# A pool of six buffers for the gates, split off from the common pool

## The chip, the cores and the metric

The kernel runs on one core of one Trainium2 chip. The metric is the time of one execution on the device, in microseconds (us). The kernel is one decoder block over 512 positions, in float32 accuracy.

## What is computed

The reference, cut to what matters here (`D_MODEL` = 1024, `D_CONV` = 1024, `D_RNN` = 1280, `D_FF` = 2816):

```python
z = rmsnorm(x, norm1_g) @ w_in + b_in
z_glu, z_rx, z_rg, z_ga, z_gb = split(z)
u = causal_conv31(glu(z_glu)); y_a = silu(layernorm(u)) @ conv_w_out + conv_b_out
xb = causal_conv4(z_rx)
r, i = sigmoid(xb @ wa + ba), sigmoid(xb @ wx + bx)      # 16 blocks of 80 x 80
log_a = -8 * r * softplus(-lam); a = exp(log_a)
h[t] = a[t] * h[t-1] + sqrt(-expm1(2 * log_a))[t] * (i * xb)[t]
y_b = (h * gelu(z_rg)) @ lru_w_out
x = x + (sigmoid(z_ga) * y_a + sigmoid(z_gb) * y_b) @ w_mix_out
h2 = rmsnorm(x, norm2_g)
x = x + (silu(h2 @ w1) * (h2 @ w3)) @ w2                 # SwiGLU
out = rmsnorm(x, norm_f_g)
```

## The kernel before, in words

**Tiles and buffers.** Activations lie channel by position, in tiles of 128 x 512 float32. Each such tile takes a buffer of the pool "long" (65 buffers, `SLOTS`) or, if it lives briefly, of "short" (5). A buffer is taken at the first write of a tile and is free again after the last read. A float32 product is made of three matmuls of rounded parts (`mm3`, line 428): every operand is split into a high part, cast on ACT (line 117), and a low part, the difference, on DVE or POOL (line 113). A split thus takes two "long" buffers (`pairt`, line 97) for one tile.

**Weights** come in chunks: a load into one of 4 raw buffers, a cast on ACT, a subtraction on POOL (for `w_in` and the gates' weights) or on DVE (for all later ones), into one of 5 buffers "hl". `weights` (line 161) emits them 4 chunks ahead of the product that uses them.

**Order.** The program states what is computed from what; a planner in the framework fixes, when the program is built, the order of the instructions on each engine, which buffer each tile takes, and the waits. It goes through the program with estimates of its own for the durations, prefers what stands earlier in the program, and lets an instruction that needs a buffer wait until one is free. On the chip each engine goes through its own list in that order.

**Stages.** (1) `norm1` and the transposes to `h1` (8 pairs of tiles, 16 buffers). (2) A list `ORDER` (line 201) mixes the input products (`z`, line 437), the gates `g0` to `g9` (`gates`, line 702), the recurrences `r0` to `r9` (`recur`, line 736) and, in steps between them, the 31 taps of the long convolution on DVE (line 596). In the list each `r` follows its `g` so that at most three gates are open: g0, g1, g2, then r0 and r1, and so on. (3) `yb`, 8 products over the 10 pairs `y`; beside them the layer norm of the convolution, and sums of weight blocks for the mixing product (`make_sums`, line 276) whose splits `mxt1k`, `mxt4k` stay in "long". (4) `ya`, and the mixing product `mx` with seven block products instead of eight (`Sevenfold`, line 806). (5) `norm2` to `h2`, then the two SwiGLU products, `f` and, for four of eleven pairs, `fr`. (6) The last product `or` (Sevenfold again, named "o", line 842), and the final norm.

**The gates.** `gates(j)` makes two products into PSUM banks `r_` and `i_`, and from them, with ACT and DVE, two tiles that outlive it, `th{j}` (line 721) and `ea{j}` (line 725). `recur(j)` reads `th{j}` in a square root on ACT (line 739) and `ea{j}` in the scan on DVE (line 741). These are "the gates' two lasting results".

**Sevenfold pairs.** For each of the 11 pairs of column blocks of the SwiGLU result, `pair(k, ua, va)` (line 821) leaves five "long" tiles: the split of `u` (`ous{k}`, two buffers), the split sum `os1p{k}`, the differences `oe{k}` (line 829) and `ov{k}`. `run` (line 842) then goes over the pairs a first time: product `k` reads `ous{k}` and `os1p{k}` (line 840), which frees three buffers, and the pair's later operands are split off, `oe{k}` to `oeb{k}` and `ov{k}` to `ovb{k}` (line 863), which takes four and frees two. These `oeb` and `ovb` are needed only in the second pass over the pairs. After pair 0 `run` also starts the loads of the residual `x2b` (8 buffers) and of the last norm's weights `gf` (2 buffers).

Of the kernel before, what the change touches and what calls it, by code (L numbers as in the profile page):

```python
# [28 lines left out]
NF = DF // P  # L29


SLOTS, SHORT = 65, 5
RAW = 4
HL = 5
AHEAD = 4
# [45 lines left out]
def tile_block(ctx, tc, a, out):  # L81
# [9 lines left out]
    def tiles(tag, bufs):  # L91
        p_ = pool(tag, bufs)
        return lambda name, dtype=F32: p_.tile([P, T], dtype, tag=tag, name=name)

    longt, shortt = tiles("long", SLOTS), tiles("short", SHORT)

    def pairt(name, dtype=F32R):

# [2 lines left out]
    def bank(name):  # L101
        return psum.tile([P, T], F32, tag="mm", name=name)
# [9 lines left out]
    def sub(eng, o, x, y):  # L112
        return eng.tensor_tensor(out=o, in0=x, in1=y, op=ALU.subtract)  # L113

    def split_to(h, l, full, eng, copy=act.copy):

        copy(h, full)  # L117
        last = sub(eng, l, full, h.bitcast(F32))
        if eng is pool_e:
            newest["sub"] = last.ins  # L120
        return h, l

    def split(name, full, eng, p_=None, copy=act.copy):
        p_ = p_ or pairt(name)
        return split_to(*p_, full, eng, copy)
# [35 lines left out]
    def weights(key, ahead=AHEAD):  # L161
        i = next(i for i, c in enumerate(chunks) if c[0] == key)
        emit_to(i + 1 + ahead)
        return held.pop(key)
# [374 lines left out]
    ab, e, s, s2, po, c4 = (sm[:, i, :] for i in range(6))  # L539
# [162 lines left out]
    def gates(j):  # L702
        hv, lv = (gate_view(v[:, 0, :]) for v in weights(f"gate{j}"))
        j5 = j % 5
        banks = []
        for g in range(2):
            ps = bank(f"g{j}_{g}")
            (wh, oh), (wl, ol) = ((v[:, g, 0, :], v[:, g, 1, :]) for v in (hv, lv))
            xh, xl = xbp[j]
            mms = [(wh, xh), (wh, xl), (wl, xh)]  # L710
            if j5 % 2:
                eh, el = ext[j]
                mms += [(l[:MANY], r[:MANY]) for l, r in ((oh, eh), (oh, el), (ol, eh))]
            else:
                mms.append((oh[: 3 * FEW], ext[j][0][: 3 * FEW]))
            for k, (l, r) in enumerate(mms):
                pe.matmul(ps, l, r, start=k == 0, stop=k == len(mms) - 1)  # L717
            banks.append(ps)

        r_, i_ = banks  # L720
        th = longt(f"th{j}")
        act.activation(th, r_, AF.Tanh, scale=0.5, bias=bh[:, 0, j : j + 1])
        act.activation(i_, i_, AF.Tanh, scale=0.5, bias=bh[:, 1, j : j + 1])  # L723

        A = longt(f"ea{j}")
        act.activation(A, th, AF.Exp, scale=c8[:, j : j + 1], bias=c8[:, j : j + 1])
        act.activation(r_, th, AF.Tanh, scale=c4[:, j : j + 1], bias=c4[:, j : j + 1])
        vec.scalar_tensor_tensor(out=r_, in0=A, scalar=1.0, in1=r_, op0=ALU.add, op1=ALU.mult)
        vec.scalar_tensor_tensor(out=xb[j], in0=i_, scalar=1.0, in1=xb[j], op0=ALU.add, op1=ALU.mult)
        vec.tensor_scalar(out=A, in0=r_, scalar1=1.0, scalar2=None, op0=ALU.add)  # L730
        vec.scalar_tensor_tensor(out=th, in0=A, scalar=1.0, in1=r_, op0=ALU.add, op1=ALU.mult)
        rec[j] = A, th

    rec = {}

    def recur(j):
        A, m2 = rec.pop(j)
        mu = bank(f"mu{j}")
        act.activation(mu, m2, AF.Sqrt, scale=-0.25)
        vec.tensor_tensor(out=mu, in0=xb[j], in1=mu, op=ALU.mult)  # L740
        vec.tensor_tensor_scan(xb[j], A, mu, 0.0, op0=ALU.mult, op1=ALU.add)  # L741
# [17 lines left out]
    for kind, j in ORDER:  # L759
        next(f_sums_steps, None)  # L760
        if kind == "u":
            glu(j)
        elif kind == "rx":
            rx(j)
            run_beside(4)
        elif kind == "g":
            gates(j)
        elif kind == "r":
            recur(j)
        elif kind == "rg":  # L770
            rg(j)
            run_beside(6)
        elif kind == "gb":
            sig(GB, j, sgb, "sgb")
            run_beside(6)
        else:
            sig(GA, j, sga, "sga")
            run_beside(8)
# [27 lines left out]
    class Sevenfold:  # L806
# [14 lines left out]
        def pair(self, k, ua, va):  # L821

            n = self.name
            u_ = split(f"{n}us{k}", ua, vec)
            s1 = shortt(f"{n}s1{k}")[:, LO]
            add(s1, va[:, LO], va[:, HI])
            sp = longt(f"{n}s1p{k}", F32R)
            split_to(sp[:, LO], sp[:, HI], s1, vec)
            e = longt(f"{n}e{k}")
            sub(vec, e[:, HI], ua[:, LO], va[:, LO])  # L830
            sub(vec, va[:, LO], s1, ua[:, LO])
            sub(vec, e[:, LO], ua[:, HI], va[:, LO])
            self.ops.append((u_, sp, e, va))
# [58 lines left out]
    for n, j in enumerate(mixq.order()):  # L892
# [3 lines left out]
        o = sga[j]  # L896
# [262 lines left out]
```

## Time and profile before

| | |
|---|---|
| median of 3 runs | 815.35 us (814.31 to 815.55) |
| the profiled execution | 816.61 us, of which its span is 814.8 us |
| mean granted TensorE clock in it | 0.993 |
| busy: PE, DVE, ACT, POOL | 801.8, 648.0, 445.2, 210.2 us |
| instructions | 11572 |

Stages, in us from the span's start, and the busy share of DVE in each, from a table of stretches:

| stretch | what runs on PE | DVE busy |
|---|---|---|
| 27 to 310 | input products and gates | 268.6 of 283.0 |
| 310 to 330 | last input products | 14.1 of 20.0 |
| 330 to 382 | `yb` | 39.9 of 52.0 |
| 382 to 426 | `ya` | 33.6 of 44.0 |
| 426 to 478 | mixing product, `h2` | 40.2 of 52.0 |
| 478 to 703 | SwiGLU | 162.4 of 225.0 |
| 703 to 748 | last product, first pass | 37.2 of 45.0 |
| 748 to 792 | its second pass | 24.5 of 44.0 |
| 792 to 815 | its third part and the end | 15.6 of 23.0 |

How to read the profile: a "busy" time is that of instructions executing; the matmuls' ends are modelled. A line of the waits names who waited for whom, the sum in us, the number of waits and the longest. A line of the timeline has the start, the duration, the engine, the source line, the operation, the tile written and those read; several alike that follow each other are merged (x3), and what ended an idle time before stands in brackets. The numbers of tiles are mostly left out by the profile (`th` for `th3`); which one it is follows from the order in the program.

### The profile page before, as it was taken

The numbers are of one execution on the slowest core, as the hardware profiler recorded it, in microseconds if no ns is written. First come the engines' busy times: TensorE is split into PE (matmuls) and PEld (weight loads), VectorE is DVE, ScalarE is ACT, GpSimd is POOL, SyncE is SP. The second block draws the span as 40 slices with busy tenths as digits, with TensorE's granted clock in tenths as the row PEclk, the third lists the DMA queues.
The fourth block names the chain that finished last, engine by engine and source line by source line (L and its number), as shares of the span: only waits on it lengthen the run. The fifth ranks groups of instructions, "written<-read, shape, count | busy, mean of one in ns | idle before, by whom it ended". The sixth has DMA issues, their size and how long they took to land.

```text
span 814.8 us, 11572 instructions
## 1 busy us (share of the span) xinstructions
PE 801.8 (98%) x4038; PEld 683.9 (84%) x4038; DVE 648.0 (80%) x1010; ACT 445.2 (55%) x627; POOL 210.2 (26%) x156
## 2 busy tenths in 40 slices
PE   8999999999999999999999999999999999999996
PEld 7988888887788888888888898999988888888885
DVE  4699899999999987787868869797866665688556
ACT  7546688777668855554336454374632233476443
POOL 3565778758665740000000042000000000000000
PEclk9999999999999999999999999999999999999998
DMA  7746466567565532358737525788778788576552
GB/s 209 192 123 163 131 186 204 169 192 194 163 190 156 167 88 65 101 174 256 234 106 245 156 92 177 243 251 262 227 237 264 251 286 283 185 261 210 173 167 104
DMA packets 183309, 153.47 MB, mean 188 GB/s; under 512 B 13799, under 2 KB 151443, under 8 KB 183251
## 3 DMA queue, kind: packets, MB, share of 16 engines
q1 hardware_dynamic: 183251, 152.73, 61.1%
q8 instruction: 32, 0.52, 0.3%
q14 instruction: 26, 0.21, 0.1%
HBM read 123.46 MB, written 26.21 MB: 184 GB/s over the span
## 4 chain that ended last, share of the span: by engine, by line
PE 92%; DVE 3%; DMA 1%; issue 1%; SPq 1%; POOL 0%; ACT 0%; POOLq 0%
PE z L437 31%; PE f L437 19%; PE or L840 13%; PE fr L1016 10%; PE yb L437 7%; PE ya L437 5%; PE mxr L840 5%; PE g L717 2%; DMA raw_in<-in_w_in_dram 1%; DVE cv L596 1%; SPq L393 1%; PE th L477 0%; DVE xb8l L113 0%; SPq L386 0%; POOL hl_in L113 0%
## 5 line engine op out<-in xcount | busy, mean ns | idle before, releaser
L596 DVE SCALAR_TENSOR_TENSOR cv<-u,par,cv 128x511 f32<-128x511 f32 (+17 forms) x240 | 162.8, 730 | 1.1 <-ACT cv L593 0.9
L113 POOL TENSOR_TENSOR hl_in<-raw_in,hl_in 128x1024 fp32r<-128x1024 f32 x52 | 125.4, 2415 | 92.7 <-ACT hl_in L117 90.2
L117 ACT CAST hl_in<-raw_in 128x1024 fp32r<-128x1024 f32 x52 | 54.2, 1043 | 10.2 <-PE z L437 6.6
L117 ACT CAST hl_f<-raw_f 128x1024 fp32r<-128x1024 f32 x28 | 29.3, 1051 | 51.4 <-DMA raw_f<-in_ffn_w_dram 37.7
L113 DVE TENSOR_TENSOR hl_f<-raw_f,hl_f 128x1024 fp32r<-128x1024 f32 x28 | 36.3, 1308 | 16.4 <-ACT hl_f L117 16.4
L990 POOL TENSOR_TENSOR hf<-h20h,h20l 128x512 f32<-128x512 f32 x1 | 1.3, 1287 | 172.4 <-DVE h20l L481 172.4
L117 ACT CAST hl_ob<-raw_ob 128x1024 fp32r<-128x1024 f32 (+1 forms) x23 | 23.4, 1016 | 38.9 <-PE or L840 18.6
L437 PE MATMUL z<-h10h,hl_in 128*128 128x512 f32 (+1 forms) x112 | 42.9, 385 | 1.5 <-DVE xb L741 1.2
L113 DVE TENSOR_TENSOR hl_ob<-raw_ob,hl_ob 128x1024 fp32r<-128x1024 f32 (+1 forms) x23 | 27.1, 1177 | 20.3 <-ACT hl_ob L117 20.2
L437 PE MATMUL z<-h11h,hl_in 128*128 128x512 f32 (+1 forms) x112 | 42.2, 378 | 0.0
L437 PE MATMUL z<-h12h,hl_in 128*128 128x512 f32 (+1 forms) x112 | 41.9, 376 | 0.0
L437 PE MATMUL z<-h15h,hl_in 128*128 128x512 f32 (+1 forms) x112 | 41.7, 374 | 0.0
L437 PE MATMUL z<-h14h,hl_in 128*128 128x512 f32 (+1 forms) x112 | 41.7, 374 | 0.0
L437 PE MATMUL z<-h13h,hl_in 128*128 128x512 f32 (+1 forms) x112 | 41.7, 374 | 0.0
L437 PE MATMUL z<-h16h,hl_in 128*128 128x512 f32 (+1 forms) x112 | 41.7, 374 | 0.0
L437 PE MATMUL z<-h17h,hl_in 128*128 128x512 f32 (+1 forms) x112 | 41.7, 374 | 0.0
L113 POOL TENSOR_TENSOR fws<-fws 128x256 f32<-128x256 f32 x48 | 36.3, 756 | 2.4
L113 DVE TENSOR_TENSOR ows<-ows,ows 128x512 f32<-128x512 f32 x22 | 15.2, 690 | 19.8 <-DMA ows<-in_ffn_w_dram 19.7
L113 DVE TENSOR_TENSOR hl_ot<-raw_ot,hl_ot 128x1024 fp32r<-128x1024 f32 (+1 forms) x17 | 20.1, 1191 | 11.8 <-ACT hl_ot L117 11.4
L117 ACT CAST hl_ot<-raw_ot 128x1024 fp32r<-128x1024 f32 (+1 forms) x17 | 17.5, 1028 | 17.2 <-PE or L840 15.5
L437 PEld LDWEIGHTS z<-h10h,hl_in 128*128 128x128 f32 x112 | 21.4, 191 | 6.3 <-ACT g L723 1.6
L437 PEld LDWEIGHTS z<-h11h,hl_in 128*128 128x128 f32 x112 | 21.4, 191 | 3.9
(905 smaller groups left out, 2582.3 us busy)
## 6 DMA issues: line engine op xcount, KB each, us to landing
raw_in<-in_w_in_dram SPq DMA_DIRECT2D x52, 512.0 KB
raw_f<-in_ffn_w_dram SPq DMA_DIRECT2D x28, 512.0 KB
ows<-in_ffn_w_dram SPq DMA_DIRECT2D x22, 512.0 KB
ot<-ows SPq DMA_DIRECT2D x44, 256.0 KB
raw_ob<-in_ffn_w_dram SPq DMA_DIRECT2D x33, 256.0 KB
raw_ot<-ot SPq DMA_DIRECT2D x33, 256.0 KB
fws<-in_ffn_w_dram SPq DMA_DIRECT2D x64, 128.0 KB
ft<-fws SPq DMA_DIRECT2D x64, 128.0 KB
```

The source lines that it names most:

```text
L113: return eng.tensor_tensor(out=o, in0=x, in1=y, op=ALU.subtract)
L117: copy(h, full)
L393: nc.sync.dma_start(xt[t][h], x_nat[:, t, h * T : (h + 1) * T])
L437: pe.matmul(ps, l, r, start=i == 0, stop=i == n - 1)
L596: vec.scalar_tensor_tensor(out=acc[c][:, s:], in0=u[c][:, : T - s], scalar=dw(c, s), in1=acc[c][:, s:], op0=ALU.mult, op1=ALU.add)
L717: pe.matmul(ps, l, r, start=k == 0, stop=k == len(mms) - 1)
L840: pe.matmul(banks[i], l_[:, ts], r_, start=start and n == 0, stop=stop and n == 2, skip_group_check=again)
L990: pool_e.tensor_tensor(out=v, in0=h2p[c][0].bitcast(F32), in1=h2p[c][1].bitcast(F32), op=ALU.add)
L1016: pe.matmul(ps[:, HALVES[i]], lw[:, 4 * i + c, :], rx_, start=not (again or i or c or m), stop=bool(i and c == 3 and m == 2), skip_group_c ...
```

## The change

`th{j}` and `ea{j}` of all ten gates are taken from a new pool "gate" of 6 buffers. "long" has 59 buffers instead of 65, so the sum stays the same. In the last Sevenfold product ("o") the difference tiles `oe0` to `oe5` are taken from "gate" too; `oe6` to `oe10`, and those of the mixing product, stay in "long". No instruction that computes or loads is added or removed.

```diff
-SLOTS, SHORT = 65, 5
+SLOTS, SHORT, GATES = 59, 5, 6
...
-    longt, shortt = tiles("long", SLOTS), tiles("short", SHORT)
+    longt, shortt, gatet = tiles("long", SLOTS), tiles("short", SHORT), tiles("gate", GATES)
...
-        th = longt(f"th{j}")
+        th = gatet(f"th{j}")
...
-        A = longt(f"ea{j}")
+        A = gatet(f"ea{j}")
...
-            e = longt(f"{n}e{k}")
+            e = (gatet if n == "o" and k < GATES else longt)(f"{n}e{k}")
```

## The prediction, made before the changed kernel was built

> **What bounds the kernel now.** I read the page first, then PE's waits, then a table of stretches around the one large gap, then the timelines of DVE and ACT at the places where buffers run short.
>
> ```profile
> PE 801.8 (98%) x4038; PEld 683.9 (84%) x4038; DVE 648.0 (80%) x1010; ACT 445.2 (55%) x627; POOL 210.2 (26%) x156
> ...
> PE 92%; DVE 3%; DMA 1%; issue 1%; SPq 1%; POOL 0%; ACT 0%; POOLq 0%
> ```
>
> PE is busy in 801.8 of 814.8 us, and 92% of the chain that ended last is PE. What PE does isn't changed. So the change can gain only where PE stands idle or slow, and lose only where it makes PE stand. PE's own waits are few; the two that fall between the start and the end are:
>
> ```profile
> PE z L437 <- DVE xb L741: 1.2, 1, 1.2
> ...
> PE g L717 <- DVE th L731: 0.6, 1, 0.6
> ```
>
> Both belong to one gap, at g7:
>
> ```profile
> 203.82 0.50 PE L717 MATMUL g<-xb7h,hl_gate 128*128 128x512 f32 x1 [0.63 <-DVE th L731]
> ...
> 206.24 0.77 PE L437 MATMUL z<-h10h,hl_in 128*128 128x512 f32 x1 [1.22 <-DVE xb L741]
> ```
>
> ```profile
> 202.80:206.20 3.40, 1.59 (x6) 0.67 (x4) 3.40 (x6) 3.36 (x6) 3.24 (x4) 1.00 0.39 111
> 206.20:209.60 3.40, 3.36 (x8) 2.71 (x9) 3.40 (x5) 3.28 (x4) 0.83 (x2) 0.50 0.42 119
> 209.60:213.00 3.40, 3.40 (x16) 2.77 (x16) 3.40 (x7) 0.00 (x0) 3.40 (x3) 1.00 0.31 79
> ```
>
> (Columns: stretch, length, busy time of PE, weight load, DVE, ACT, POOL, granted clock, DMA.) In the first row PE is idle for 3.40 - 1.59 = 1.81 us; in the second the granted clock is 0.50. There 8 matmuls start; at the 0.227 us that lie between two starts elsewhere (209.96, 210.19) 15 fit, so 7 x 0.227 = 1.6 us more are lost. The gap costs 1.8 + 1.6 = 3.4 us in all, the most that a better order could give back in the middle of the kernel.
>
> The Trainium skill (TensorE: Matmul & The Clock Gate, Part 1) has the clock fall to half after an idle window of about 3.4 us. The rows differ: PE was busy for 1.59 us of the 3.40 us before it fell. By the page a new gap of two or three us would cost its own length alone; by the rows up to 1.6 us more.
>
> **The change part by part.** No instruction and no byte is added, so the only terms are waits for buffers. I counted the buffers of "long" in use from each tile's first write to its last read in the trace. Where the count without the tiles that move stays at 59 or less, the new limit doesn't bite, whatever the planner does.
>
> *The gates' six buffers.* The ten pairs live, in us: th0 and ea0 74 to 111, th1 and ea1 91 to 117, th2 and ea2 115 to 160, th3 and ea3 124 to 162, th4 and ea4 140 to 206, th5 and ea5 161 to 207, th6 and ea6 192 to 246, th7 and ea7 204 to 247, th8 and ea8 237 to 270, th9 and ea9 257 to 272. Single tiles end earlier, at the square roots of line 739. Never more than six live at once; six are reached at 142 (ea4), 195 (ea6) and 240 (ea8). The closest reuse is th7, which starts at 204.4 on ACT after th4 was read for the last time at 201.0, by an instruction earlier in ACT's own list. Cost: 0. Gain: also 0, since before there were free buffers for all of them (at most 55 of 65 in use up to 300 us). The list up to 300 us should therefore stay as it is, with its gap.
>
> *59 buffers from 300 to 382.* Here the count reaches 60 in two places. First, sga4, sga5 and sga6 at 310.8, 316.1 and 322.1: 16 of h1, 20 of y, 8 each of sgb and u, the sga so far, and up to 3 of the layer norm. They would wait for the layer norm's split (until 311.0), its column sum (316.6) and the first matmuls of the last input product, which free h1 (322.5 to 322.7): 0.2, 0.5 and 0.6 us, on ACT. Behind sga5 is a chunk's cast at 317.2 whose chunk PE uses only at 334.6, ready 13.4 us early. Cost: 0, hidden by that lead. Second:
>
> ```profile
> 369.51 0.82 DVE L113 TENSOR_TENSOR hl_lo<-raw_lo,hl_lo 128x640 fp32r<-128x640 f32 x1
> 370.24 0.69 DVE L113 TENSOR_TENSOR mxt41l<-mxws,mxt41h 128x512 fp32r<-128x512 f32 x1
> 370.84 0.69 DVE L785 TENSOR_TENSOR sgb<-yb,sgb 128x512 f32<-128x512 f32 x1
> 373.88 1.23 DVE L113 TENSOR_TENSOR hl_co<-raw_co,hl_co 128x1024 fp32r<-128x1024 f32 x1 [2.35 <-ACT hl_co L117]
> ```
>
> mxt41l is the 60th tile (y 20, un 16, sgb 8, sga 8, mxt 8). With 59 it waits for the first y to be read out, in the last yb product, at 376.0: 5.8 us. The operand itself isn't needed before 459. Best case, the planner puts other DVE work first: 0. Worst case, DVE stands with the `sgb` product and the first `co` chunk behind it. That chunk is then done at 376.0 + 0.69 + 0.60 + 1.23 = 378.5 instead of 375.1; PE first uses it at 382.2. A lead of 3.7 us is left, so 0 in the worst case too. The raw buffer that mxt41l reads is held 5.8 us longer; it is one of four, the next mixing load waits for it, and the next chunk (`co1`) slips from 375.1 to some 377, with 11 us of lead. Cost: 0.
>
> *478 to 707.* All six of oe0 to oe5 live from 599 to 707.6, and 59 + 6 = 65. The pressure there (65 of 65 at 698, where oe9 waits for h2 to be freed) is the same before and after: 0.
>
> *707 to 748, the place that counts.* Once oe0 to oe5 are split, the six buffers are empty and nobody else may have them, while "long" is still full. From 719 the count without oe0 to oe5 is 60 to 64:
>
> ```profile
> 721.24 0.69 DVE L113 TENSOR_TENSOR ovb3l<-ov,ovb3h 128x512 fp32r<-128x512 f32 x1
> 721.84 1.22 DVE L113 TENSOR_TENSOR hl_ob<-raw_ob,hl_ob 128x1024 fp32r<-128x1024 f32 x1
> ...
> 734.22 0.69 DVE L113 TENSOR_TENSOR ovb8l<-ov,ovb8h 128x512 fp32r<-128x512 f32 x1
> ...
> 738.90 0.69 DVE L113 TENSOR_TENSOR ovb10l<-ov,ovb10h 128x512 fp32r<-128x512 f32 x1
> 740.66 1.23 DVE L113 TENSOR_TENSOR hl_ob<-raw_ob,hl_ob 128x1024 fp32r<-128x1024 f32 x1 [1.08 <-ACT hl_ob L117]
> 743.35 1.23 DVE L113 TENSOR_TENSOR hl_ot<-raw_ot,hl_ot 128x1024 fp32r<-128x1024 f32 x1 [1.47 <-ACT hl_ot L117]
> ```
>
> With a products of the first pass done (one each 4.09 us from 702.6; two of the three buffers come free at two thirds) and s pairs split, "long" holds 59 - 3a + 3s up to s = 6, and 65 - 3a + 2s from there; a split needs up to four more in pairs 0 to 5, three more afterwards. So the last split of pairs 3, 4, 5 can start at 721.7, 725.8, 729.9 instead of 721.2, 725.5, 728.2; pairs 6 to 10 end about 0, 1.6, 3.1, 1.0 and 2.5 us later. None of these is needed before 748. What stands behind them on DVE and ACT are the chunks of PE's next products, ready 4.1 to 5.6 us early in 719 to 744 (the smallest: done at 723.1, used at 727.1), and the first `ot` chunk, done at 744.6 and used at 747.5: 2.9 us. Each single delay is at most 3.1 us where 4.1 are left, and 2.5 us at the end. Best case 0; worst case, the delays add up, 0.5 + 0.3 + 1.7 + 0 + 1.6 + 3.1 + 1.0 + 2.5 = 10.7 us. DVE is free for 20.5 - 18.72 = 1.8 us in 719.1 to 739.6 and for 8.2 - 5.67 = 2.5 us up to 747.8; with the lead of 2.9 us that covers 7.2, and 3.5 us reach PE, with the clock's fall 5.1. I take 0, since splits wait for the same PE products that free the chunks' buffers, so the delays should overlap rather than add.
>
> **The sum** is 0 + 0 + 0 + 0: 816.6 us for the profiled execution. The median of the runs shown is 1.3 us lower, and the forecast is against it: 815.4 us.
>
> **The rivals.**
> *Delays that add up (slower).* In the first pass of the last product the planner's list puts splits ahead of chunks, and DVE, which goes through it in order, stands for each. For it: it is the only long stretch with "long" over 59, and leads there are small. Against it: the arithmetic above. It decides once DVE stands for more than 7.2 us between 719 and 748. Price 3.5 us: 818.9. The Trainium skill (TensorE: Matmul & The Clock Gate, Architectural detail) calls ACT and DVE strict FIFO; the trace of before has nothing against it.
> *Another order (slower).* Waits at 310 to 376 make the planner list things differently later on, where leads are thinnest: the chunk done at 532.1 has 1.2 us, one at 528.7 has 1.7. One DVE instruction of 1.23 us or two in front of them costs up to some 2 us: 817.4. Against it: the list between 427 and 684 has buffers to spare.
> *The gap at g7 goes (faster).* Its two releasers, lines 731 and 741, work on the very tiles that move, and DVE started g6's line 728 only at 200.7, 3.9 us after its last input had been written (ACT, 196.7). If the own pool shifts that, 3.4 us go: 812.0. Against it: six buffers are enough, so nothing is planned otherwise.
> *The change does nothing*, because no limit binds where it matters, is the forecast itself.
>
> **How the numbers follow.** No difference 0.60; delays that add up 0.16; another order 0.10; the gap goes 0.14. Faster by over 0.2% (about what a measurement of this kernel can tell from no change, 1.6 us) is 0.14, within it 0.60, slower 0.26. Leaving out the faster case and the upper half of the first rival would leave out 0.22, so the range goes from 812.0 to 818.9, and the likeliest case's own from 813.8 to 817.0.
>
> **What would show it.** Right: PE's waits still hold the two at g7, and the timelines of PE before 300 us are the same; mxt41l comes after 376 on DVE; ovb10l comes after 742; PE has no gap in 703 to 748. Wrong: a wait of PE for a `hl_ob` or `hl_ot` chunk in 719 to 750; a granted clock of 0.50 in a new place, or none at 206; a last y, sga or mxt split that a chunk waits behind. The forecast falls with the claim that the list up to 300 us stays as it was.

## The result, and the profile after

The changed kernel takes 818.83 us (median of 6 runs, 817.72 to 821.25); the kernel before, run beside it, 814.7 us (median of 6). The ratio is 1.0052, 95% interval 1.0037 to 1.0068: **slower by half a per cent, 4.2 us** (ratio less 1, times 814.7). The forecast was no difference. The profiled execution took 817.72 us, its span is 815.9 us.

The page of the changed kernel, its busy times and its chain of work:

```profile
PE 801.4 (98%) x4038; PEld 684.7 (84%) x4038; DVE 645.8 (79%) x1010; ACT 442.9 (54%) x625; POOL 210.7 (26%) x156
...
PE 84%; DVE 5%; DMA 3%; SPq 2%; ACT 2%; POOL 2%; issue 1%; POOLq 0%; ACTq 0%
```

PE's busy time is the same to 0.4 us, but 84% of the chain is PE where it was 92%: somewhere the work of the other engines now holds PE up. PE's waits between 27 and 815 us are only these (engine and line that waited, releaser, us in total, times, longest):

```profile
PE g L718 <- DMA ext<-xb6h: 4.4, 1, 4.4
PE f L438 <- ACT h20h L481: 0.3, 1, 0.3
```

The second of them stood in before too. Both waits at g7 are gone, and there is a new one at g5. (Lines of the changed kernel are one higher: 718 is 717 of before.) The table of stretches shows both places, with the columns as in the prediction: around g5, then around g7.

```profile
156.10:159.50 3.40, 2.81 (x13) 2.00 (x11) 3.40 (x7) 3.37 (x6) 3.40 (x3) 1.00 0.44 119
159.50:162.90 3.40, 0.00 (x0) 0.00 (x0) 3.40 (x5) 2.50 (x3) 3.32 (x3) 1.00 0.31 68
162.90:166.30 3.40, 3.00 (x7) 2.45 (x8) 3.40 (x6) 1.24 (x2) 3.24 (x4) 0.57 0.16 32
202.80:206.20 3.40, 3.40 (x17) 2.82 (x16) 3.40 (x6) 1.80 (x3) 3.22 (x3) 1.00 0.94 288
206.20:209.60 3.40, 3.40 (x17) 2.78 (x16) 3.40 (x6) 2.44 (x4) 2.82 (x4) 1.00 0.25 69
```

In the second row PE does nothing at all; in the third it runs at a granted clock of 0.57 and starts seven matmuls in 3.4 us. To see what such a place costs, take the start of one and the same matmul in two traces and follow the difference from 41 us (from here to g5 PE goes in step in all runs) to 792 us (the last product's third part). Against a run further below in which PE has no gap between 41 us and the 0.3 us for h20h (g49), PE of the changed kernel falls back by 6.2 us at g5 and by 0.2 us at 538 us, where the runs differ by up to 0.7 us: **6.5 us** in all, of which 4.4 us are the wait and the rest mostly the slow clock behind it. The profiled execution of before falls back by 4.1 us, all of it at g7. I call this sum PE's lateness.

What makes g5 wait are the small copies `ext<-xb6` (line 697 of before). SP's queue in the trace of before, and then in that of the changed kernel:

```profile
149.46 2.38 SPq L188 DMA_DIRECT2D raw_gate<-in_lru_wa_dram  x5
151.89 2.55 SPq L188 DMA_DIRECT2D raw_gate<-in_lru_wx_dram  x5
154.55 0.54 SPq L697 DMA_DIRECT2D ext<-xb6h  x1
155.19 0.54 SPq L697 DMA_DIRECT2D ext<-xb6l  x1
155.78 1.22 SPq L697 DMA_DIRECT2D ext<-xb6h  x2
```

```profile
154.02 0.41 SPq L145 DMA_DIRECT2D raw_in<-in_w_in_dram  x1
156.50 2.31 SPq L189 DMA_DIRECT2D raw_gate<-in_lru_wa_dram  x5
158.85 1.04 SPq L189 DMA_DIRECT2D raw_gate<-in_lru_wx_dram  x2
160.01 0.54 SPq L698 DMA_DIRECT2D ext<-xb6h  x1
160.64 0.54 SPq L698 DMA_DIRECT2D ext<-xb6l  x1
161.23 1.21 SPq L698 DMA_DIRECT2D ext<-xb6h  x2
```

g5 needs the first three copies; the others are for g7. In the changed kernel the third is issued at 161.23 and PE goes on at 163.29: 2.06 us. In before it was issued at 155.78, so if it took as long it had landed by 157.84, and PE used it at 159.98: 2.1 us to spare. The copies are issued 5.46 us later (154.55 to 160.01), and PE comes to g5 1.23 us earlier in this profile: 5.46 + 1.23 - 2.1 = 4.6 us of waiting, and 4.4 are seen. Right ahead of the copies SP stands from 154.43 to 156.50, for POOL's memset of the buffer that the gate's loads go to (155.94 to 156.47), and then issues seven of these loads. And the copied tile itself is late on DVE, in before and after:

```profile
152.42 1.34 DVE L113 TENSOR_TENSOR xb6l<-xb,xb6h 128x512 fp32r<-128x512 f32 x1
```

```profile
156.26 0.69 DVE L114 TENSOR_TENSOR xb6l<-xb,xb6h 128x512 fp32r<-128x512 f32 x1
```

DVE is busy in 123.9 of the 131 us from 27 to 158 us before, and in 124.2 after. It does `xb6l` as its 238th instruction instead of its 232nd: six more of the long convolution's steps stand ahead.

The memset and the seven loads can't be the whole reason. The run g49 has both (SP stands 2.1 us for that memset), and no wait at g5:

```profile
150.01 2.31 SPq L188 DMA_DIRECT2D raw_gate<-in_lru_wa_dram  x5
152.36 1.04 SPq L188 DMA_DIRECT2D raw_gate<-in_lru_wx_dram  x2
153.52 0.54 SPq L697 DMA_DIRECT2D ext<-xb6h  x1
```

In the changed kernel SP comes to this place late already. The tile before, xb5, is late on DVE by the same six places (217th instead of 211th; before, then after), and SP stands for its two halves, the last two lines, where before it stood 0.6 us:

```profile
138.38 0.70 DVE L113 TENSOR_TENSOR xb5l<-xb,xb5h 128x512 fp32r<-128x512 f32 x1
```

```profile
143.31 0.69 DVE L114 TENSOR_TENSOR xb5l<-xb,xb5h 128x512 fp32r<-128x512 f32 x1
```

```profile
SPq L698 <- ACT xb5h L118: 3.9, 1, 3.9
SPq L698 <- DVE xb5l L114: 1.2, 1, 1.2
```

So DVE's order seems to reach g5 twice, through xb6 and through SP's queue. The first difference in any list lies much earlier, at th1 and th2 on ACT. Before, and after:

```profile
91.25 0.68 ACT L722 ACTIVATE th<-g,bh 128x512 f32<-128x512 f32 x1
114.53 0.69 ACT L722 ACTIVATE th<-g,bh 128x512 f32<-128x512 f32 x1
```

```profile
85.11 0.69 ACT L723 ACTIVATE th<-g,bh 128x512 f32<-128x512 f32 x1 [0.19 <-PE g L718]
104.59 0.69 ACT L723 ACTIVATE th<-g,bh 128x512 f32<-128x512 f32 x1
```

### The profile page after: what moved, and what is told of

Same layout as the page of the kernel before. It is cut to its first block, busy times and chain, and to the rows that moved or that the text cites. A ratio compares the mean times of both kernels' runs of the same rounds, so it can differ in the third digit from the quotient of the medians.

```text
span 815.9 us, 11578 instructions
## 1 busy us (share of the span) xinstructions
PE 801.4 (98%) x4038; PEld 684.7 (84%) x4038; DVE 645.8 (79%) x1010; ACT 442.9 (54%) x625; POOL 210.7 (26%) x156
## 4 chain that ended last, share of the span: by engine, by line
PE 84%; DVE 5%; DMA 3%; SPq 2%; ACT 2%; POOL 2%; issue 1%; POOLq 0%; ACTq 0%
PE z L438 24%; PE f L438 19%; PE or L841 13%; PE fr L1017 10%; PE yb L438 7%; PE ya L438 5%; PE mxr L841 5%; DVE cv L597 3%; DMA raw_in<-in_w_in_dram 2%; PE g L718 1%; POOL hl_in L114 1%; SPq L394 1%; SPq L189 1%; ACT hl_in L118 0%; DVE xb L675 0%
## 5 line engine op out<-in xcount | busy, mean ns | idle before, releaser
L597 DVE SCALAR_TENSOR_TENSOR cv<-u,par,cv 128x511 f32<-128x511 f32 (+16 forms) x240 | 162.5, 730 | 2.3 <-ACT cv L594 2.2
L675 DVE SCALAR_TENSOR_TENSOR xb<-z,par,xb 128x511 f32<-128x511 f32 (+2 forms) x30 | 22.3, 743 | 4.1 <-ACT xb L673 3.9
```

Of the source, the lines that this page charges most:

```text
L597: vec.scalar_tensor_tensor(out=acc[c][:, s:], in0=u[c][:, : T - s], scalar=dw(c, s), in1=acc[c][:, s:], op0=ALU.mult, op1=ALU.add)
L675: vec.scalar_tensor_tensor(out=o[:, s:], in0=ps[:, : T - s], scalar=lw(s), in1=o[:, s:], op0=ALU.mult, op1=ALU.add)
```

## The experiments

**The theory.** With a pool of their own, the gates' tiles no longer wait for a turn in the common pool. Their work moves forward in the planner's lists, other work on DVE and SP moves back, and g5 waits. **The rivals**: 59 buffers instead of 65 cost the time, later on; or any use of the second pool does; or DVE alone makes the copies late, without SP. (Edits are shown against the changed kernel, those of sgb_own and xb_own against the kernel before.)

### Which part of the change costs the time

Two kernels with half of the change each. `e_only` leaves the gates in the common pool:

```diff
-        th = gatet(f"th{j}")
+        th = longt(f"th{j}")
...
-        A = gatet(f"ea{j}")
+        A = longt(f"ea{j}")
```

> Only oe0 to oe5 use the pool of six; th and ea of all gates are in the common pool, which has 59 buffers. Up to 300 us the instructions are in the order of before. Theory (the gates' own pool changes the order of the work before 300 us, and that costs the time): as before, ratio 1.000, PE's two waits at g7 are there (1.8 us), no wait at g5. Rival (59 buffers instead of 65, and late splits, cost it): ratio 1.005 as in the changed kernel.

Measured: 1.0012 (1.0002 to 1.0022), PE's waits at g7 as before, none at g5. `gates_only` is the other half:

```diff
-            e = (gatet if n == "o" and k < GATES else longt)(f"{n}e{k}")
+            e = longt(f"{n}e{k}")
```

> Only th and ea of the gates use the pool of six; all differences oe stay in the common pool of 59. Up to 300 us the order is that of the changed kernel. Theory (order before 300 us): ratio 1.005, with PE's wait of 4 us at g5 for the copies of xb6; whatever the last product loses with six buffers fewer comes on top and shows as waits of PE after 700 us. Rival (59 buffers cost it): no wait at g5, and a loss after 700 us alone.

Measured: 1.0044 (1.0027 to 1.0060), a wait of 4.3 us at g5, no wait after 700 us. So the gates' part is the cost. The rest, the smaller common pool and the oe in the new one, costs 1 us (0.2 to 1.8 us by the interval) where nothing was expected. The profile of e_only loses 0.6 us at 538 us, beside a wait of 0.3 us for a result of ACT; but g49 loses nothing there, though its lists are the same from 221 us on. What this 1 us is stays open.

### The pool kept, the order put back

`order_back` is the changed kernel, with each th queued on ACT behind the result that it followed in before:

```diff
-        act.activation(th, r_, AF.Tanh, scale=0.5, bias=bh[:, 0, j : j + 1])
+        with tc.issue_after(long_on_act[-1]):
+            act.activation(th, r_, AF.Tanh, scale=0.5, bias=bh[:, 0, j : j + 1])
```

(`long_on_act` collects the ACT instructions that write sgb, xbh and yh.)

> The changed kernel with one thing added: the first ACT instruction of each gate's th is queued behind the newest sgb, xbh or yh result on ACT, the place it had before; the pool of six stays. Theory (the order costs the time, not the pool): no wait at g5, ratio 1.000 if the gap at g7 comes back, 0.996 if it doesn't (3.4 to 4.1 us less). Rival (the pool's size and the late splits): ratio 1.005.

Measured: 1.0001 (0.9985 to 1.0017). th2 is back at 112.0 us (114.5 in before, 104.6 in the changed kernel) and PE no longer waits at g5 for the copies of xb6. The gap at g7 didn't come back either, but the ratio isn't the 0.996 expected for that case: two small waits, 0.2 us behind g5 and 0.9 us at g6, took its place. PE's lateness is 2.4 us. The order costs the time; a cost of the pool alone doesn't show, and by the interval it is 1.4 us at most.

### Which gate

The change for some gates alone, all with oe0 to oe5 in the pool of six; for instance `g12`:

```diff
-        th = gatet(f"th{j}")
+        th = (gatet if j in (1, 2) else longt)(f"th{j}")
...
-        A = gatet(f"ea{j}")
+        A = (gatet if j in (1, 2) else longt)(f"ea{j}")
```

> The change for th1, ea1, th2, ea2 alone (with oe0 to oe5 in the pool of six and 59 common buffers); the other gates stay in the common pool. Theory (the earlier places of g1's and g2's work on ACT and DVE push xb3 to xb6 back by 4 to 6 us, and this alone makes g5 wait): a wait of some 4 us at g5 for the copies of xb6, ratio 1.005 if the gap at g7 goes with it, 1.010 if it stays. Rival (the later gates make the difference, or all together): no wait at g5, ratio 1.000.

> The change for g4 to g9 alone (with oe0 to oe5); g0 to g3 stay in the common pool. Theory: up to g4 the order is that of before, so no wait at g5; ratio 1.000 if the gap at g7 stays, 0.995 to 0.996 if the earlier work of g4 and g6 removes it. Rival (the pool of six costs time wherever it is used): over 1.004.

> The change for g6 to g9 alone (with oe0 to oe5). th6 and ea6 come on ACT ahead of the casts of hl_in25 and xb8h instead of behind them. Theory: the gap at g7, which waited for th of g6 and then for the scan of the recurrences behind it, goes: PE's two waits there (1.8 us) vanish with the half clock behind them, ratio 0.995 to 0.996. Rival (the gap at g7 hangs on the long convolution's steps and DVE's load, not on g6's place): the waits stay, ratio 1.000.

> The change for th1 and ea1 alone (with oe0 to oe5 in the pool of six and 59 common buffers). Theory (g5 waits because xb6 comes too late in DVE's list): xb6l is DVE's 230th instruction here (before: 232nd, changed kernel: 238th), so g5 doesn't wait; ratio 1.000 if the gap at g7 stays, 0.997 if it goes. Rival (any earlier gate makes g5 wait): a wait of some 4 us at g5, ratio 1.004.

> The change for th2 and ea2 alone (with oe0 to oe5 in the pool of six and 59 common buffers). Theory: xb6l is DVE's 241st instruction here (before: 232nd, changed kernel: 238th), so g5 waits at least as long as in the changed kernel, 4 to 6 us, the gap at g7 is gone since PE comes there later by that, ratio 1.004 to 1.006. Rival (it needs g1 and g2 together): no wait at g5, ratio 1.000.

| own pool for | ratio | interval | wait at g5, us | waits at g7, us | PE's lateness, us |
|---|---|---|---|---|---|
| g1, g2 | 1.0039 | 1.0027 to 1.0051 | 3.7 | none | 5.6 |
| g2 | 1.0045 | 1.0031 to 1.0060 | 3.9 | none | 6.1 |
| g1 | 0.9982 | 0.9973 to 0.9992 | 0.3 | none | 1.3 |
| g4 to g9 | 0.9969 | 0.9957 to 0.9981 | none | none | 0 (the run compared with) |
| g6 to g9 | 0.9972 | 0.9961 to 0.9983 | none | none | 0.6 |

One pair of tiles, th2 and ea2, does all the harm: with `xb6l` as DVE's 241st instruction g5 waits, with it as the 230th (g1) only 0.3 us are left. The harm pays one bill, though: in g12 the order of DVE at g6 and g7 is that of before, but PE comes there 5.5 us later, and DVE is ready by then. This can be why the gap at g7 is gone in the changed kernel as well, paid at g5 at a higher price; there g6's work is earlier too, as in the next runs, and which of the two did it isn't shown.

And where only later gates have the pool, the gap at g7 goes and nothing comes in its place. `g49` takes 812.07 us, **faster than both kernels**: 2.5 us less than before, and by the two ratios 6.8 us less than the changed kernel. In the trace of g49 th of g6 is done on DVE 11.8 us earlier than in before (191.35 for 203.10; 1.5 us of it come from the start), and the scans of the recurrences follow:

```profile
191.35 0.68 DVE L731 SCALAR_TENSOR_TENSOR th<-ea,g 128x512 f32<-128x512 f32 x1
...
199.61 2.32 DVE L741 TENSOR_TENSOR_SCAN xb<-ea,mu 128x512 f32<-128x512 f32 x2
```

### SP's queue, or DVE alone

`ext_first`: the changed kernel with the loads of `raw_gate6` behind the copies.

```diff
-                            nc.sync.dma_start(v[r : r + nr, gi, ei, c : c + ncol], a[name][0, h + 8 * (j // 5), hr : hr + nr, hc : hc + ncol])
+                            gate_load(j, v[r : r + nr, gi, ei, c : c + ncol], a[name][0, h + 8 * (j // 5), hr : hr + nr, hc : hc + ncol])
...
+    def gate_load(j, o, i):
+        if j == 6 and "ext" in newest:
+            with tc.issue_after(newest["ext"]):
+                nc.sync.dma_start(o, i)
+        else:
+            nc.sync.dma_start(o, i)
```

> The changed kernel with one thing added: on SP the loads of the seventh gate's weights (raw_gate6, ten DMAs) are queued behind the copies ext<-xb6, where the changed kernel has seven of them ahead. ACT and DVE keep the changed kernel's order but for two or three neighbours. Theory (the copies are late because SP gets to them 3.4 us late behind those loads, after 2 us in which it stood for their memset): xb6l is done at 157.0, the third copy is issued at 157.5 and landed 2 us later, so PE's wait at g5 falls from 4.4 to some 0.7 us, and since the gap at g7 is gone too, the ratio is 0.998 (813 us). Rival (DVE's later xb6 alone is enough, the queue adds little): the wait stays over 3 us, ratio 1.004.

Measured: 1.0071 (1.0055 to 1.0088), a wait of 5.4 us. **The expectation failed.** The planner put another load into the place that came free, and SP stood 4.7 us for that one, for a buffer that POOL was still reading; its queue in ext_first:

```profile
154.32 5.51 SPq L144 DMA_DIRECT2D raw_in<-in_w_in_dram  x2
159.94 0.54 SPq L704 DMA_DIRECT2D ext<-xb6h  x1
```

The third copy, issued at 161.15, then took 3.4 us until PE went on, where it had taken 2.06.

`ext_first3` puts that load, `raw_in29`, behind the copies as well (the same `issue_after`, around the loads of both chunks):

> The changed kernel with one thing added: on SP the loads of raw_gate6 and of raw_in29 (in the run before it was this load that stood ahead of the copies, until 159.5 us) are both queued behind the copies ext<-xb6. Theory (SP's queue makes the copies late): the first copy is issued as soon as xb6h is there, at 155, the third after xb6l, at 157.5, landed 2 us later; PE's wait at g5 falls to 0.7 us or less, and the ratio is 0.998 unless another product now waits for weights that are loaded later (then the loss stands at that product). Rival (DVE's later xb6 is enough by itself): the wait stays over 3 us and the ratio at 1.004.

Measured: 1.0050 (1.0034 to 1.0066). PE's waits between 27 and 320 us in ext_first3:

```profile
PE z L443 <- POOL hl_in L113: 3.1, 2, 2.8
PE g L723 <- DMA ext<-xb6h: 0.9, 1, 0.9
PE g L723 <- DVE y1l L113: 0.4, 1, 0.4
```

At g5 the copies now cost 0.9 us instead of 4.4, with `xb6l` still DVE's 238th instruction: SP's queue was the larger part of the wait. But nothing is gained. A chunk of the next products, loaded later, now makes PE wait 2.85 us at 210 us, with half the clock behind it. Around this wait, from 203.90 to 214.07, DVE is busy in 10.14 and POOL in 9.86 of 10.17 us: there is little room for anything that comes late.

SP's earlier standing for xb5 goes with the loss. Where PE waits 3.7 us or more at g5, SP has stood 5.1 to 6.2 us for the two halves of xb5; in the runs without such a wait it stood 2.3 us at most, except in ext_first3 (5.2), where the copies go ahead. In g2, g12 and xb_own SP doesn't stand for the memset at all. No run moves xb5 alone, so this link is read off the traces and not tested.

### Why an own pool moves th1 and th2

At th1 and th2 the common pool had free buffers (the prediction counted at most 55 of 65 in use). So it isn't room that they waited for. Two other splits of the pool test the turn. `sgb_own` gives the eight sgb a pool (8 buffers, 57 left, oe0 to oe7 there too), and leaves the gates alone:

```diff
-        dest[j] = longt(f"{name}{j}")
+        dest[j] = (sgbt if name == "sgb" else longt)(f"{name}{j}")
```

> The kernel before with another pool split off instead: the eight sgb tiles (with oe0 to oe7) have eight buffers of their own, th and ea stay in the common pool, which has 57. Theory (a tile with an own pool no longer waits for its turn behind tiles that stand earlier in the program): sgb1 comes on ACT ahead of the cast xb3h instead of behind it, some 5 us earlier, while th1 and th2 keep their places; xb6l is DVE's 232nd instruction as before, so no wait at g5; ratio 1.000, or 0.997 if the gap at g7 goes. Rival (only the gates' tiles matter, their place is set by something else than the pool): sgb1 keeps its place.

Measured: sgb1 does come ahead of the cast xb3h, at 84.3 us instead of 90.7; th1 keeps its place behind both. But the ratio is 1.0029 (1.0017 to 1.0042), not 1.000: `xb6l` is DVE's 232nd instruction as expected, yet DVE does it at 155.3 us, 2.8 us later than in before; PE waits 1.1 us at g5 for the copies, and in the next product 1.3 us for a scan. The place in the list was right, the time was not. The same 231 instructions stand ahead of `xb6l`, but DVE stands for POOL's part of a gate's weights, which in before it doesn't:

```profile
124.53 0.81 DVE L193 CAST hl_gate<-raw_gate 32x256 fp32r<-32x256 f32 x1 [2.76 <-POOL hl_gate L113]
```

So a place in a list says when something comes only together with the waits ahead of it.

`xb_own` takes away what stands ahead of th1 and th2 in the program, the pairs xbh, xbl and the copies ext, into a pool of ten (with sga and oe later); th and ea stay in the common pool:

```diff
-        p_ = pairt(f"xb{j}")
+        p_ = xbt(f"xb{j}h", F32R), xbt(f"xb{j}l", F32R)
...
-                    ext[key] = pairt(f"ext{key}") if j5 % 2 else (longt(f"ext{key}", F32R),)
+                    ext[key] = (xbt(f"ext{key}h", F32R), xbt(f"ext{key}l", F32R)) if j5 % 2 else (xbt(f"ext{key}", F32R),)
```

> The kernel before with the opposite split: the pairs xbh and xbl and the copies ext (later sga and the differences oe) have a pool of ten buffers, and th and ea stay in the common pool, which has 55. Theory (in the common pool th1 and th2 stand behind the turn of xb3's and xb4's pairs and copies, which stand earlier in the program): with those taken out, th1 and th2 come early on ACT (86 and 105 us) as in the changed kernel, though they have no pool of their own; xb6l is DVE's 236th instruction (before 232nd, changed kernel 238th), and g5 waits 2 to 4 us for the copies of xb6, ratio 1.002 to 1.004. Rival (the gates' own pool moves them, not the turn): th1 at 91 and th2 at 114 us, no wait at g5, ratio 1.000.

Measured: 1.0051 (1.0034 to 1.0068), more than the 1.002 to 1.004 expected, and a wait of 3.9 us at g5. `xb6l` is the 236th. th1 and th2 on ACT in xb_own:

```profile
85.60 0.69 ACT L722 ACTIVATE th<-g,bh 128x512 f32<-128x512 f32 x1
105.00 0.68 ACT L722 ACTIVATE th<-g,bh 128x512 f32<-128x512 f32 x1
```

These are the changed kernel's places and its loss, without a pool for the gates. So th1 and th2 come early as soon as they don't share a pool with tiles that stand earlier in the program, whichever of the two is moved out. That the planner hands out a pool's buffers in the order of the program, free buffers or not, fits every list here; it was read off the lists, not off the planner.

### The gap at g7, once more

> The kernel before once more, unchanged, for a second profile. In its first profile PE came out of the gap at g7 4.1 us late, with the granted clock at 0.50 for 3.4 us behind it; in the run where only oe0 to oe5 use the pool of six, the same gap cost 2.5 us, at a clock of 1.00. Theory (whether the clock falls after this gap varies from execution to execution of the same kernel): either is possible, 2.5 or 4.1 us, nothing between. Rival (it goes with the kernel): 4.1 us and 0.50 again.

Measured: one time of 814.58 us, and a lateness of 2.5 us, of which 2.1 us at g7 (a little less than either value expected). There are two waits as before, 0.4 and 1.2 us, and no slow clock behind them; the two stretches in before_again:

```profile
202.80:206.20 3.40, 1.78 (x7) 1.10 (x7) 3.40 (x5) 3.36 (x5) 3.32 (x3) 1.00 0.37 104
206.20:209.60 3.40, 3.40 (x17) 2.77 (x16) 3.40 (x6) 2.80 (x4) 0.84 (x2) 1.00 0.35 91
```

So the same gap costs 4.1 us in one execution of the same kernel and 2.1 us in another, 2.5 us in e_only. The median of before, 814.7 us, lies by the second execution (814.58) and not by the first (816.61), so I take its lateness of 2.5 us for before. With it the lateness explains the times. PE's lateness less 2.5 us, beside the measured difference (ratio less 1, times 814.7 us):

| kernel | lateness less 2.5, us | measured, us |
|---|---|---|
| the changed kernel | 4.0 | 4.2 |
| gates_only | 3.7 | 3.6 |
| e_only | 0.6 | 1.0 |
| order_back | -0.1 | 0.1 |
| g12 | 3.1 | 3.2 |
| g2 | 3.6 | 3.7 |
| g1 | -1.2 | -1.5 |
| g69 | -1.9 | -2.3 |
| g49 | -2.5 | -2.5 |
| ext_first | 6.7 | 5.8 |
| ext_first3 | 4.4 | 4.1 |
| xb_own | 5.1 | 4.2 |
| sgb_own | 1.3 | 2.4 |

All agree within 1.1 us, ten within 0.4: the places where PE falls back account for the effect, as far as these profiles, one for each kernel, can tell.

## Why the prediction was wrong, point by point

The time, 818.83 us, lies just inside the range, which ends at 818.9. That is luck: this end was the price of splits that stand ahead of chunks in the last product, and nothing was lost there. As a difference, the 4.2 us measured are more than the 3.5 us of that price.

- **What bounds the kernel** was right: PE, with its busy time unchanged, and all that changed is where PE stands. (The prediction leaves out a third wait, of 0.3 us for h20h, which stands in both kernels.)
- **The gates' six buffers** is the step that failed: "Where the count without the tiles that move stays at 59 or less, the new limit doesn't bite, whatever the planner does", and from it "The list up to 300 us should therefore stay as it is, with its gap". Gain and cost were put at 0 because free buffers were there; the count was right and beside the point. The order depends on which tiles share a pool, even while ten of its 65 buffers are free; the lists differ from th1 on. With it fell cost 0 and gain 0: the runs show 6.2 us lost at g5, and the gap at g7 gained (2.5 us of lateness in before, 4.1 in its first profile).
- **59 buffers from 300 to 382**: cost 0 was right (e_only, and no wait of PE here). The three sga come 0.3, 0.7 and 0.8 us later, after PE's own shift of 0.9 us, for 0.2, 0.5 and 0.6 predicted. mxt41l came at 379.9 where 376.0 was given: the planner put the first two `co` chunks and the last `sgb` product ahead of it, the best case named there.
- **478 to 707**: 0, right as far as the profiles tell. The changed kernel loses 0.2 us at 538 us; g49 and g1, whose lists are the same there, lose 0 and 0.7 us.
- **707 to 748**: cost 0 was right; PE is busy in 45.00 of 45.00 us. The last splits of pairs 3, 4 and 5 start at 722.9, 726.9 and 731.1, less the shift of 0.9 us at 722.0, 726.0 and 730.2, for 721.7, 725.8 and 729.9 predicted. The last of pair 10 comes at 750.6, 11 us later than before and not 2.5, since the planner let chunks go first. So the arithmetic of the buffers held for pairs 3 to 5; the rival "delays that add up" needed splits ahead of chunks, and towards the end the opposite was done.
- **The rivals.** "The gap at g7 goes" came true, and it was given as a gain of 3.4 us; alone, in g49 and g69, it is worth 2.5 and 2.3 us. Its reason against, "six buffers are enough, so nothing is planned otherwise", is the failed step again. "Another order" was the right kind of mechanism in the wrong place: it was looked for after 427 us, out of waits for buffers. The place where leads are thin and the first list difference were never put together: DVE is busy 95% from 27 to 310 us, so a change of order there can make a later product's operands late.
- **What would show it** named it: the forecast falls with the list before 300 us, and a granted clock near one half in a new place was the sign.
- **The clock.** "Up to 1.6 us more" than the gap's own length was the right size (4.1 against 2.5 us), and it comes or doesn't: of three profiles with the gap at g7 the clock fell in one, and behind the waits at g5 of 3.7 us and more it fell every time, in six profiles. A single wait of 2.85 us (ext_first3) was followed by it too; PE fell back by 4.8 us there, near the 2.85 + 1.6 that the prediction's rows would give. The Trainium skill (TensorE: Matmul & The Clock Gate, Part 1) has the window of some 3.4 us run freely, not starting anew with the kernel; that the same gap is followed by half the clock in one execution and not in another agrees with it.

## What to carry to other kernels

A buffer pool is part of the order of the work, not only of its memory: before you take an edit to pools as neutral, compare the lists of every engine with and without it, from the first tile that moves, and don't count buffers alone. Where an engine is as busy as DVE here (95%), a piece that moves forward moves others back; look for the product with the thinnest lead behind it, the small copies and the queue that issues them included. A pool split that loses as a whole can win in part: here g4 to g9 alone gain 0.3%, and g2 alone costs 0.45%.

## What the runs showed of the hardware

- The same gap of PE, waits of 0.4 to 0.6 and 1.2 us within 3.4 us, was followed by a granted clock of 0.50 in one profile and of 1.00 in two (before_again, e_only). At g7 PE lost 4.1, 2.1 and 2.5 us; even at full clock that is 0.5 to 0.7 us more than the waits add up to.
- An SP queue in which one transfer waits holds back all behind it, whoever needs them: 3.9 and 1.2 us for the halves of xb5 and 2.1 us for a memset in the changed kernel, and in ext_first, with 4.7 us of standing, two loads take 5.5 us to issue where two took 1.2 us elsewhere (168.26 in the changed kernel). The Trainium skill (DMA: Bandwidth & Descriptors, Anatomy of one DMA) has any wait for a semaphore happen on the engine that issues a transfer, before it is handed on; the rows agree.
- A copy of 32 rows of 2 KB inside SBUF took 2.06 to 2.13 us from its issue until PE could go on at g5, in six traces in which PE waited for it, and 2.28 us in ext_first3. It took 3.41 us in ext_first and 3.55 us in g1, the two in which SP had issued a load of 512 KB right ahead of the copies.
